# A hybrid attention block with a convolutional feed-forward part: which engine does which copies and subtractions ahead of the feed-forward part

## The chip, the core and the metric

The kernel runs on one core of a Trainium2 chip. A core has TensorE (PE, matrix products), VectorE (DVE), ScalarE (ACT), GpSimd (POOL) and a queue for data transfers (SP). Each engine works through its own list of instructions in order and waits on semaphores where it needs another engine's result. The metric is the device time of one launch in microseconds, as a median of several launches.

## What is computed

One transformer layer on 2048 tokens of width 1024, in fp32. The part that the change touches lies ahead of the second half (the feed-forward part):

```python
h = rmsnorm(x, g_mix) * (1 + scale1) + shift1
a_u, a_v, b_q, b_k, b_v, c_q, c_k, c_v = split(h @ w_in)
y_a = spatial_gating(a_u, a_v)          # gelu, rmsnorm of v, causal 128x128 mix
y_b = stick_breaking(b_q, b_k, b_v)     # 6 heads
y_c = dilated_window(rope(c_q), rope(c_k), c_v)   # 6 heads, dilations 1, 4, 16
x = x + (1 + gate1) * (concat(y_a, y_b, y_c) @ w_out)
# then: h2 = rmsnorm(x), conv(h2 @ w_up), silu(gate) * val, @ w_down, final rmsnorm
```

Stick-breaking, for one query and all keys before it, needs a product from the far end, taken with a scan:

```python
beta = sigmoid(z);  stay = sigmoid(-z)          # both masked: beta 0, stay 1 where key >= query
weight[k] = beta[k] * prod(stay[j] for j > k)   # the stick-breaking product
out = weight @ v
```

## The kernel before

Every fp32 product on TensorE is made of three passes: an operand is split into a rounded high part (`hi`) and the rest (`lo = x - hi`), and hi·hi, hi·lo and lo·hi are added in PSUM (`mm3`, lines 90 to 104). So each weight tile, each normalised activation and each attention weight costs a cast (`copy`, lines 70 to 74) and a subtraction (`tt`, line 78) on some engine besides the matmuls.

Which engine does it is a table, `ENGINES`: each place in the code ("site") has a string of letters, `a` for ScalarE, `v` for VectorE, `p` for GpSimd, and `engine()` goes round that string with each call. `"wlo": "pvv"` puts the first of every three low parts of `w_in` tiles on GpSimd and two on VectorE.

The work goes through these stages:

- 0 to 145 us: the first modulation columns (`ada_first`: `ada_acc` sums on VectorE, line 187), the first normalised tokens (`hh`, `hl`) and the first projections (`whi`, `wlo`).
- 145 to 545 us: projections of the first 1024 tokens, the rotary embedding (`rotate`: `stage*cos`, `stage*sin`, `rot`) and the stick-breaking heads of the first half, interleaved; the spatial gating (`sgu`: `v`, `vs`).
- 545 to 805 us: the same projections of the second half and the dilated-window heads.
- 805 to 1240 us: the stick-breaking heads of the second half, with the output projection of the first half between them (`wo_hi`, `wo_lo`, `yraw`, `yh`, `yl`).
- 1240 us to the end: the rest of the output projection and the feed-forward part.

One step of `stick` on 128 queries and 512 keys: TensorE makes `z`; ScalarE makes `stay` and `beta` by two sigmoids (lines 532, 533); on the diagonal GpSimd masks both (`affine_select`, line 536); VectorE scans `stay` into `excl` (line 540); GpSimd multiplies `beta` by `excl` (site `beta`); TensorE transposes that into PSUM (`tr`, line 546); ScalarE casts it to `wh`, VectorE subtracts to `wl`; TensorE multiplies both with the values (`av`, line 557).

The order of instructions on an engine is that of a scheduler that lays the program out by its own estimates of durations. It is given the table, so a different engine for one site moves instructions on all engines. Inside `run`, side units (`~bqk2`, `~op0` and so on) are mixed into the stick heads by credit; this isn't touched.

Of the kernel before, what the change touches and what calls it, by code (L numbers as in the profile page):

```python
# [43 lines left out]
class Kernel:  # L44
# [16 lines left out]
    def engine(self, site):  # L61

        turns = ENGINES.get(site, site)
        n = self.turn[site] = self.turn.get(site, -1) + 1
# [1077 lines left out]
        self.cp.release()  # L1142


ENGINES = {"whi0": "a", "wlo0": "pppv", "lnt0": "a", "hlo0": "pppv", "lnt": "va", "lnx00": "avv", "lnx01": "aav", "lnx10": "v", "lnx11": "v", "lnx": "va", "hlo": "pvv", "whi": "v", "wlo": "pvv", "qkhi": "avv", "qklo": "v", "cqk": "a", "rot1": "ppv", "rot2": "pv", "rot3": "v", "rothi": "aav", "rotlo": "pvv", "sgu1": "pv", "sgu2": "p", "sguhi": "ap", "sgulo": "ppv", "ya": "aaav", "fold": "a", "beta": "p", "whi_s": "a", "whi_d": "avv", "wom": "v", "wohi": "aav", "wolo": "pv", "ysc": "pv", "yhi": "av", "ylo": "pv", "wuhi": "v", "wulo": "pvv", "wdm": "p", "wdhi": "av", "wdlo": "ppv", "upc": "av", "gv": "pppv", "ghi": "ap", "glo": "ppv", "vhi": "av", "vlo": "v", "uc": "v"}

BUFS = {"gm": 3, "z": 2, "tr": 2, "av": 1, "wraw": 2, "whi": 3, "wlo": 3, "s8": 3, "cs": 2, "tmp2": 2, "khat": 3, "vhat": 2, "q": 2, "beta": 4, "excl": 4, "wh": 2, "wl": 2, "fold": 1, "ys": 1, "x4": 2, "yraw": 2, "ysc": 4, "yh": 2, "yl": 2, "xo": 3, "wuraw": 4, "wul": 3, "wuh": 3, "wdraw": 2, "fx": 2, "up": 3, "dn": 5, "wdh": 2, "wdl": 2, "upc": 3, "cv": 3, "gh": 4, "gl": 4, "fs": 4, "fry": 2, "frr": 2}

# [41 lines left out]
```

## Time and profile before

| | us |
|---|---|
| median of 3 runs (2830.4 to 2834.19) | 2831.44 |
| profiled execution, its own time | 2831.72 |
| span of that execution | 2830.0 |
| PE busy | 2639.5 (93%) |
| DVE busy | 2182.7 (77%) |
| POOL busy | 1197.3 (42%) |
| ACT busy | 987.6 (35%) |

A busy time is summed over the engine's instructions, and a matmul's end is modelled. An instruction that is blocked after it has begun counts as busy all the while, so a duration can be that of the work or that of the work and a stall; the least and the median duration of one shape tell the two apart.

### The profile page before, as it was taken

What the parts mean: (1) busy time and instruction counts of PE and PEld (TensorE: products, weight loads), DVE (VectorE), ACT (ScalarE), POOL (GpSimd) and SP (SyncE); (2) the same over time, 40 slices, a digit from 0 to 9 for tenths busy, and PEclk for the clock granted to TensorE, in tenths of its full rate; (3) what the DMA queues carried; (4) which work ended last, traced back from release to release, by engine and by line L of the source; (5) the groups of instructions that cost most, each with busy time, mean ns of one, the idle gap of its engine ahead of it and who ended that gap; (6) DMA issues with size and microseconds to landing.
All of it is one profiled execution on the core that took longest, in us unless ns stands there. A gap on an engine that the chain in (4) does not pass through costs nothing.

```text
span 2830.0 us, 37108 instructions
## 1 busy us (share of the span) xinstructions
PE 2639.5 (93%) x13334; PEld 2208.6 (78%) x13334; DVE 2182.7 (77%) x3188; ACT 987.6 (35%) x1841; POOL 1197.3 (42%) x1138
## 2 busy tenths in 40 slices
PE   7989899899887888899999999999998999999997
PEld 6868897788866777777788888888877888888886
DVE  5587888766589999964787777777888778777776
ACT  5244444333455666633222112122262212112113
POOL 3276524330158776722444333334444333433323
PEclk9989999999988999999999999999999999999999
DMA  7645485878564332258211111111133111111111
GB/s 233 198 114 164 140 292 173 225 186 215 141 179 127 93 93 66 79 180 297 67 55 50 52 46 45 45 45 53 47 117 119 45 45 60 45 53 45 45 38 60
DMA packets 305300, 309.40 MB, mean 109 GB/s; under 512 B 65516, under 2 KB 245596, under 8 KB 305116
## 3 DMA queue, kind: packets, MB, share of 16 engines
q1 hardware_dynamic: 305116, 307.02, 36.8%
q8 instruction: 106, 1.74, 0.3%
q14 instruction: 78, 0.64, 0.1%
HBM read 232.36 MB, written 68.30 MB: 106 GB/s over the span
## 4 chain that ended last, share of the span: by engine, by line
PE 62%; DVE 15%; DMA 9%; issue 6%; POOL 4%; ACT 3%; SPq 1%; DVEq 0%; POOLq 0%; ACTq 0%
PE up L93 11%; PE up L94 11%; PE up L92 11%; PE dn L94 5%; PE dn L92 5%; PE dn L93 5%; DVE excl L540 3%; PE gmv L342 2%; POOL beta L78 2%; DMA wraw<-in_w_in_dram 2%; PE av L557 2%; SPq L83 1%; DMA wada<-in_w_ada_dram 1%; DVE wl L78 1%; PE tr L546 1%
## 5 line engine op out<-in xcount | busy, mean ns | idle before, releaser
L92 PE MATMUL up<-gh,wuh 128*128 128x512 f32 x1408 | 552.8, 393 | 2.1 <-ACT gh L260 2.1
L94 PE MATMUL up<-gh,wul 128*128 128x512 f32 x1408 | 554.5, 394 | 0.0
L93 PE MATMUL up<-gl,wuh 128*128 128x512 f32 x1408 | 554.3, 394 | 0.0
L821 DVE TENSOR_TENSOR acc<-dn,acc 128x512 f32<-128x512 f32 x688 | 441.4, 681 | 104.3 <-PE dn L94 103.6
L779 DVE SCALAR_TENSOR_TENSOR cv<-upc,cw,cv 128x512 f32<-128x512 f32 x352 | 339.9, 966 | 104.1 <-ACT cv L777 101.0
L78 POOL TENSOR_TENSOR beta<-beta,excl 128x128 f32<-128x128 f32 (+2 forms) x240 | 310.8, 1308 | 140.7 <-DVE excl L540 101.1
L92 PEld LDWEIGHTS up<-gh,wuh 128*128 128x128 f32 x1408 | 264.7, 188 | 62.0 <-ACT gh L260 2.3
L93 PEld LDWEIGHTS up<-gl,wuh 128*128 128x128 f32 x1408 | 265.0, 188 | 61.2 <-issue 0.2
L94 PEld LDWEIGHTS up<-gh,wul 128*128 128x128 f32 x1408 | 264.8, 188 | 59.8 <-issue 0.2
L92 PE MATMUL dn<-wdh,gh 128*128 128x512 f32 x688 | 271.3, 395 | 11.6 <-DVE acc L821 10.4
L93 PE MATMUL dn<-wdl,gh 128*128 128x512 f32 x688 | 271.2, 394 | 0.0
L94 PE MATMUL dn<-wdh,gl 128*128 128x512 f32 x688 | 256.6, 396 | 0.0
L777 ACT ACTIVATE cv<-up,cb 128x512 f32<-128x512 f32 x176 | 136.6, 776 | 284.6 <-DVE upc L72 284.6
L540 DVE TENSOR_TENSOR_SCAN excl<-stay,excl 128x513 f32<-128x513 f32 x144 | 224.6, 1574 | 2.0 <-ACT stay L532 1.9
L70 ACT ACTIVATE upc<-up 128x512 f32<-128x512 f32 x88 | 52.5, 597 | 379.7 <-PE up L94 379.6
L70 ACT ACTIVATE wh<-tr 128x128 fp32r<-128x128 f32 (+2 forms) x240 | 128.5, 541 | 161.2 <-PE tr L546 150.4
L72 DVE CAST wuh<-wuraw 128x512 fp32r<-128x512 f32 x176 | 131.3, 785 | 63.5 <-PE up L93 58.3
L546 PE MATMUL tr<-ident,beta 128*128 128x128 f32 x816 | 139.4, 292 | 37.1 <-POOL beta L78 26.5
L342 PE MATMUL gmv<-wlo,hh 128*128 128x256 f32 x576 | 169.5, 295 | 2.5 <-DVE wlo L78 1.4
L774 POOL COPY upc<-upc 128x2 f32<-128x2 f32 x88 | 20.7, 235 | 353.6 <-DVE upc L72 302.2
L342 PE MATMUL gmv<-whi,hh 128*128 128x256 f32 x576 | 169.0, 294 | 1.3 <-DVE vst L78 1.3
L78 POOL TENSOR_TENSOR wlo<-wraw,whi 128x512 fp32r<-128x512 f32 x35 | 53.4, 1529 | 275.2 <-DVE whi L72 178.3
(249 smaller groups left out, 6092.5 us busy)
## 6 DMA issues: line engine op xcount, KB each, us to landing
wuraw<-in_w_up_dram SPq DMA_DIRECT2D x176, 256.0 KB, 3.2
wdraw<-in_w_down_dram SPq DMA_DIRECT2D x44, 512.0 KB, 3.5
wada<-in_w_ada_dram SPq DMA_DIRECT2D x32, 512.0 KB, 5.7
wraw<-in_w_in_dram SPq DMA_DIRECT2D x112, 128.0 KB, 4.7
vd<-vst SPq DMA_DIRECT2D x12, 1024.0 KB, 5.3
q<-bq SPq DMA_DIRECT2D x48, 256.0 KB, 4.3
q<-cq SPq DMA_DIRECT2D x48, 256.0 KB, 4.2
x<-xo SPq DMA_DIRECT2D x24, 512.0 KB, 6.0
```

Of the source, the lines that this page charges most:

```text
L70: self.nc.scalar.activation(out, in_, AF.Copy)
L72: self.nc.vector.tensor_copy(out, in_)
L78: (self.nc.vector if eng == "v" else self.nc.gpsimd).tensor_tensor(out=out, in0=a, in1=b, op=op)
L92: self.nc.tensor.matmul(ps, ah, bh, start=(k == 0), stop=False)
L93: self.nc.tensor.matmul(ps, ah, bl, start=False, stop=False)
L94: self.nc.tensor.matmul(ps, al, bh, start=False, stop=(k == n - 1))
L342: self.nc.tensor.matmul(ps[:, e, :], a[:, o:o + P], b, start=(n == 0), stop=(n == 3 * KB - 1))
L540: nc.vector.tensor_tensor_scan(x[:, o:513][:, ::-1], sr, sr, 1.0 if diag else carry[j], op0=ALU.mult, op1=ALU.bypass)
L546: nc.tensor.transpose(tr[:, e, :], b[:, o + e * P:o + (e + 1) * P], self.ident)
L777: nc.scalar.activation(t, ps, AF.Identity, bias=self.cb[:, blk:blk + 1], scale=self.cw[2][:, blk:blk + 1])
L779: nc.vector.scalar_tensor_tensor(out=t, in0=u[:, tap:tap + TG], scalar=self.cw[tap][:, blk:blk + 1], in1=t, op0=ALU.mult, op1=ALU.add)
L821: nc.vector.tensor_tensor(out=acc[t][:, ns], in0=ps, in1=acc[t][:, ns], op=ALU.add)
```

## The change

One line of the table is changed. Sites used ahead of the feed-forward part that had some or all of their calls on GpSimd go to VectorE altogether (`wlo0`, `hlo0`, `hlo`, `wlo`, `rot1`, `rot2`, `rotlo`, `sgu1`, `sgu2`, `sgulo`, `wolo`, `ysc`, `ylo`), and two casts to ScalarE (`whi`, which was on VectorE, and `sguhi`). `beta` stays on GpSimd, and so do the masks, which name GpSimd in the code. The sites of the feed-forward part itself (`wulo`, `wdm`, `wdlo`, `gv`, `ghi`, `glo`) stay; `hlo` is also used for the normalised rows that enter it.

```diff
-ENGINES = {"whi0": "a", "wlo0": "pppv", "lnt0": "a", "hlo0": "pppv", ..., "hlo": "pvv", "whi": "v", "wlo": "pvv", ..., "rot1": "ppv", "rot2": "pv", "rot3": "v", "rothi": "aav", "rotlo": "pvv", "sgu1": "pv", "sgu2": "p", "sguhi": "ap", "sgulo": "ppv", ..., "wolo": "pv", "ysc": "pv", "yhi": "av", "ylo": "pv", ...}
+ENGINES = {"whi0": "a", "wlo0": "v", "lnt0": "a", "hlo0": "v", ..., "hlo": "v", "whi": "a", "wlo": "v", ..., "rot1": "v", "rot2": "v", "rot3": "v", "rothi": "aav", "rotlo": "v", "sgu1": "v", "sgu2": "v", "sguhi": "a", "sgulo": "v", ..., "wolo": "v", "ysc": "v", "yhi": "av", "ylo": "v", ...}
```

In all 117 instructions leave GpSimd: 35 `wlo`, 25 `hl` and `gl`, 14 `stage` and 4 `rot` of the rotary embedding, 11 of the spatial gating, 12 `yraw`, 12 `yl` and 4 `wo_lo`. 115 of them come to VectorE and 2 to ScalarE, and 76 casts `whi` go from VectorE to ScalarE.

GpSimd's list in the first half's stick heads, near 210 us (names carry the number of their tile; `cos` is the table of the rotary embedding), before:

```order
L78 TENSOR_TENSOR beta_1611<-beta_1611,excl_1618 128x384
L536 AFFINE_SELECT stay0_676<-stay0_676 128x128
L536 AFFINE_SELECT beta_1630<-beta_1630 128x128
L78 TENSOR_TENSOR beta_1630<-beta_1630,excl_1637 128x512
L78 TENSOR_TENSOR stage_2550<-stage_2550,cos_1403 128x1024
L78 TENSOR_TENSOR beta_1660<-beta_1660,excl_1663 128x512
L78 TENSOR_TENSOR rot_2609<-rot_2609 128x1024
L536 AFFINE_SELECT stay0_676<-stay0_676 128x128
L536 AFFINE_SELECT beta_1715<-beta_1715 128x128
L78 TENSOR_TENSOR beta_1676<-beta_1676,excl_1679 128x512
```

and the same stretch of GpSimd's list now:

```order
L78 TENSOR_TENSOR beta_1611<-beta_1611,excl_1618 128x384
L536 AFFINE_SELECT stay0_676<-stay0_676 128x128
L536 AFFINE_SELECT beta_1630<-beta_1630 128x128
L78 TENSOR_TENSOR beta_1630<-beta_1630,excl_1637 128x512
L78 TENSOR_TENSOR beta_1660<-beta_1660,excl_1663 128x512
L78 TENSOR_TENSOR beta_1676<-beta_1676,excl_1679 128x512
L536 AFFINE_SELECT stay0_676<-stay0_676 128x128
```

The two 1024-wide instructions that stood between the products of one group are gone, and its three products follow each other.

VectorE's list where the output projection's weights are made, near 835 us (`excl` is the scan, `wl` the low part of the attention weights), before:

```order
L540 SCALAR_TENSOR_TENSOR excl_8872<-stay1_678,excl_8827 128x513
L78 TENSOR_TENSOR woraw_8535<-woraw_8535,gate2_8518 128x1024
L78 TENSOR_TENSOR wl_8765<-tr_8798,wh_8764 128x4x128
L78 TENSOR_TENSOR yraw_8637<-ycraw_8650,yscale_8649 128x4x64
L540 SCALAR_TENSOR_TENSOR excl_8888<-stay2_680,excl_8843 128x513
L78 TENSOR_TENSOR wl_8820<-tr_8830,wh_8819 128x4x128
L78 TENSOR_TENSOR wl_8820<-tr_8846,wh_8819 128x4x128
L78 TENSOR_TENSOR wo_lo1_8539<-woraw_8535,wo_hi1_8538 128x1024
L540 SCALAR_TENSOR_TENSOR excl_8935<-stay0_676 128x129
```

and from the same scan on now:

```order
L540 SCALAR_TENSOR_TENSOR excl_8872<-stay1_678,excl_8827 128x513
L78 TENSOR_TENSOR woraw_8535<-woraw_8535,gate2_8518 128x1024
L78 TENSOR_TENSOR wl_8765<-tr_8798,wh_8764 128x4x128
L78 TENSOR_TENSOR yraw_8637<-ycraw_8650,yscale_8649 128x4x64
L540 SCALAR_TENSOR_TENSOR excl_8888<-stay2_680,excl_8843 128x513
L78 TENSOR_TENSOR wo_lo0_8532<-woraw_8528,wo_hi0_8531 128x1024
L78 TENSOR_TENSOR wl_8820<-tr_8830,wh_8819 128x4x128
L540 SCALAR_TENSOR_TENSOR excl_8935<-stay0_676 128x129
L78 TENSOR_TENSOR wl_8820<-tr_8846,wh_8819 128x4x128
L540 SCALAR_TENSOR_TENSOR excl_8952<-stay1_678 128x257
L78 TENSOR_TENSOR wo_lo1_8539<-woraw_8535,wo_hi1_8538 128x1024
```

`wo_lo0`, which GpSimd made, now stands in VectorE's list behind a scan and ahead of the `wl` that the next `av` matmuls need.

ScalarE's list in the first stick heads (a piece of the difference, with + for now and - for before; `whi` is a cast of a `w_in` tile, `wh` the cast of the transposed attention weights):

```order
+L70 ACTIVATE whi<-wraw 128x512 x2
+L70 ACTIVATE wh<-tr 128x2x128
+L533 ACTIVATE beta<-z 128x256
+L70 ACTIVATE wh<-tr 128x3x128
+L532 ACTIVATE stay_676<-z 128x512
+L533 ACTIVATE beta<-z 128x512
+L70 ACTIVATE whi<-wraw 128x512 x2
+L532 ACTIVATE stay_678<-z 128x512
```

The casts of the weights now stand in pairs between the sigmoids and the `wh` casts of the stick heads.

## Rows read from the trace of the kernel before

**Rows 1.** Windows: stretch, length, busy of PE, PEld, DVE, ACT, POOL; clock, DMA, GB/s.

```profile
0.00:145.00 145.00, 121.21 (x635) 103.12 (x636) 85.28 (x136) 57.56 (x99) 45.29 (x92) 0.98 0.70 211
145.00:545.00 400.00, 361.74 (x2347) 328.68 (x2346) 325.88 (x457) 169.12 (x327) 197.14 (x169) 0.95 0.62 186
545.00:805.00 260.00, 233.76 (x1530) 211.88 (x1529) 163.15 (x435) 102.47 (x263) 47.21 (x38) 0.95 0.67 172
805.00:1240.00 435.00, 368.62 (x2060) 302.28 (x2060) 388.05 (x411) 258.90 (x530) 310.70 (x285) 0.93 0.38 105
1240.00:2830.00 1590.00, 1554.20 (x6768) 1262.59 (x6766) 1220.39 (x1750) 399.55 (x624) 596.97 (x555) 0.99 0.23 72
```

**Rows 2.** The same for the inner part of the fourth stretch.

```profile
845.00:1200.00 355.00, 301.94 (x1723) 249.03 (x1724) 330.30 (x348) 224.69 (x462) 269.86 (x248) 0.94 0.33 93
```

**Rows 3.** PE's waits, 805 to 1240 us: us in total, times, longest.

```profile
PE tr L546 <- POOL beta L78: 26.5, 34, 2.2
PE av L557 <- DVE wl L78: 22.7, 20, 2.6
```

**Rows 4.** Instruction groups of POOL, 145 to 545 us: busy us, mean ns | idle before.

```profile
L78 POOL TENSOR_TENSOR wlo<-wraw,whi 128x512 fp32r<-128x512 f32 x15 | 23.3, 1550 | 82.1 <-DVE whi L72 60.6 <-PE z L528 10.3 <-DMA stage<-stage 5.9
L78 POOL TENSOR_TENSOR stage<-stage,cos 128x1024 f32<-128x1024 f32 x7 | 21.4, 3053 | 15.8 <-DMA stage<-stage 8.1 <-ACT cos L381 7.7
...
L78 POOL TENSOR_TENSOR stage<-stage,sin 128x1024 f32<-128x1024 f32 x5 | 14.0, 2801 | 19.6 <-DMA q<-cq 15.7 <-DMA stage<-stage 3.9
```

**Rows 5.** The group of DVE that goes to ACT, 145 to 545 us.

```profile
L72 DVE CAST whi<-wraw 128x512 fp32r<-128x512 f32 x43 | 30.8, 741 | 1.4 <-DMA wraw<-in_w_in_dram 1.4
```

**Rows 6.** The cast that ACT does already, whole span.

```profile
L70 ACT ACTIVATE whi<-wraw 128x512 fp32r<-128x512 f32 x12 | 7.2, 626 | 16.4 <-DMA wraw<-in_w_in_dram 16.3
```

**Rows 7.** Three tiles' instructions on DVE, whole span: ns least/median/most, first and last start.

```profile
L78 DVE TENSOR_TENSOR wlo<-wraw,whi x53: 658/681/2260, 31.4 to 775.5; 128x512 fp32r<-128x512 f32 x53
...
L72 DVE CAST whi<-wraw x76: 394/426/2635, 98.2 to 775.2; 128x512 fp32r<-128x512 f32 x76
...
L78 DVE TENSOR_TENSOR stage<-stage,sin x6: 1187/1266/2830, 174.5 to 593.6; 128x1024 f32<-128x1024 f32 x6
```

**Rows 8.** Timeline, DVE and POOL, 8 to 60 us: start us, us.

```profile
14.75 0.75 DVE L187 SCALAR_TENSOR_TENSOR ada_acc<-wada,cact,ada_acc 128x512 f32<-128x512 f32 x1
...
20.47 11.05 DVE L187 SCALAR_TENSOR_TENSOR ada_acc<-wada,cact,ada_acc 128x512 f32<-128x512 f32 x7
...
19.26 4.18 POOL L78 TENSOR_TENSOR wlo<-wraw,whi 128x512 fp32r<-128x512 f32 x3 [13.51 <-ACT whi L70]
```

**Rows 9.** Chain of waits: start us, us, what.

```profile
209.99 4.89 POOL stage L78
...
791.27 2.41 POOL v L78
```

**Rows 10.** Instruction groups of POOL that move, 805 to 1240 us.

```profile
L78 POOL TENSOR_TENSOR yraw<-ycraw,yscale 128x256 f32<-128x256 f32 x11 | 16.4, 1493 | 23.4 <-DVE yl L78 15.2 <-DMA yscale<-scd 6.1 <-issue 1.2
...
L78 POOL TENSOR_TENSOR yl<-yraw,yh 128x1024 fp32r<-128x1024 f32 x4 | 11.4, 2851 | 0.0
L78 POOL TENSOR_TENSOR wo_lo<-woraw,wo_hi 128x1024 fp32r<-128x1024 f32 x4 | 10.9, 2720 | 0.6 <-DVE wo_hi L72 0.6
```

**Rows 11.** Instruction groups of DVE, 805 to 1240 us.

```profile
L540 DVE TENSOR_TENSOR_SCAN excl<-stay,excl 128x513 f32<-128x513 f32 x120 | 189.8, 1597 | 0.2 <-ACT stay L532 0.2
...
L78 DVE TENSOR_TENSOR yraw<-ycraw,yscale 128x256 f32<-128x256 f32 x10 | 9.4, 938 | 0.0
...
L78 DVE TENSOR_TENSOR wo_lo<-woraw,wo_hi 128x1024 fp32r<-128x1024 f32 x4 | 7.4, 1856 | 0.0
...
L78 DVE TENSOR_TENSOR yl<-yraw,yh 128x1024 fp32r<-128x1024 f32 x4 | 5.7, 1433 | 0.0
```

**Rows 12.** Tile `excl`, 805 to 1240 us: ns least/median/most.

```profile
L78 POOL TENSOR_TENSOR beta<-beta,excl x168: 408/1096/2493, 811.6 to 1213.0; 128x512 f32<-128x512 f32 x132, 128x128 f32<-128x128 f32 x12, 128x256 f32<-128x256 f32 x12, 128x384 f32<-128x384 f32 x12
L540 DVE TENSOR_TENSOR_SCAN excl<-stay,excl x120: 1252/1506/3386, 812.1 to 1211.5; 128x513 f32<-128x513 f32 x120
```

More of the change, by code (lines that the diff above doesn't have):

```diff
@@ L1142, in run @@
         self.cp.release()
-ENGINES = {"whi0": "a", "wlo0": "pppv", "lnt0": "a", "hlo0": "pppv", "lnt": "va", "lnx00": "avv", "lnx01": "aav", "lnx10": "v", "lnx11": "v", "lnx": "va", "hlo": "pvv", "whi": "v", "wlo": "pvv", "qkhi": "avv", "qklo": "v", "cqk": "a", "rot1": "ppv", "rot2": "pv", "rot3": "v", "rothi": "aav", "rotlo": "pvv", "sgu1": "pv", "sgu2": "p", "sguhi": "ap", "sgulo": "ppv", "ya": "aaav", "fold": "a", "beta": "p", "whi_s": "a", "whi_d": "avv", "wom": "v", "wohi": "aav", "wolo": "pv", "ysc": "pv", "yhi": "av", "ylo": "pv", "wuhi": "v", "wulo": "pvv", "wdm": "p", "wdhi": "av", "wdlo": "ppv", "upc": "av", "gv": "pppv", "ghi": "ap", "glo": "ppv", "vhi": "av", "vlo": "v", "uc": "v"}
+ENGINES = {"whi0": "a", "wlo0": "v", "lnt0": "a", "hlo0": "v", "lnt": "va", "lnx00": "avv", "lnx01": "aav", "lnx10": "v", "lnx11": "v", "lnx": "va", "hlo": "v", "whi": "a", "wlo": "v", "qkhi": "avv", "qklo": "v", "cqk": "a", "rot1": "v", "rot2": "v", "rot3": "v", "rothi": "aav", "rotlo": "v", "sgu1": "v", "sgu2": "v", "sguhi": "a", "sgulo": "v", "ya": "aaav", "fold": "a", "beta": "p", "whi_s": "a", "whi_d": "avv", "wom": "v", "wohi": "aav", "wolo": "v", "ysc": "v", "yhi": "av", "ylo": "v", "wuhi": "v", "wulo": "pvv", "wdm": "p", "wdhi": "av", "wdlo": "ppv", "upc": "av", "gv": "pppv", "ghi": "ap", "glo": "ppv", "vhi": "av", "vlo": "v", "uc": "v"}
 BUFS = {"gm": 3, "z": 2, "tr": 2, "av": 1, "wraw": 2, "whi": 3, "wlo": 3, "s8": 3, "cs": 2, "tmp2": 2, "khat": 3, "vhat": 2, "q": 2, "beta": 4, "excl": 4, "wh": 2, "wl": 2, "fold": 1, "ys": 1, "x4": 2, "yraw": 2, "ysc": 4, "yh": 2, "yl": 2, "xo": 3, "wuraw": 4, "wul": 3, "wuh": 3, "wdraw": 2, "fx": 2, "up": 3, "dn": 5, "wdh": 2, "wdl": 2, "upc": 3, "cv": 3, "gh": 4, "gl": 4, "fs": 4, "fry": 2, "frr": 2}
```

## The prediction

> **What bounds the kernel now.** I read first the busy time of the engines by stretch [rows 1]. After 1240 us TensorE is busy for 1554 of 1590 us: matmuls bound that half, and nothing in it but eleven `gl` is moved. Ahead of it TensorE is idle for 24, 38, 26 and 66 us in the four stretches (length less busy time), 154 us together. That is the most that the change can win at the clock granted there; in the fourth stretch that clock is 0.93 of 2.4 GHz.
>
> Then the waits of TensorE in the fourth stretch [rows 3]: 26.5 us for GpSimd's product `beta`, 22.7 us for VectorE's `wl`. So one engine that loses work and one that gains work hold TensorE up about equally. The inner part shows how full they are: VectorE is busy for 330 of 355 us (93%), GpSimd for 270 (76%) [rows 2]. In the second stretch VectorE is busy for 326 of 400 us, GpSimd for 197, ScalarE for 169 [rows 1].
>
> Last I read durations, since "busy" hides stalls here. One `ada_acc` sum takes 0.75 us alone, and seven take 11.05 us, 1.58 each, while GpSimd runs its `wlo` and `hl` [rows 8]. The cast `whi` has a median of 426 ns over the whole span and a mean of 741 in the second stretch, where GpSimd is busiest beside it [rows 5, 7]. The scan has a least time of 1252 ns and a mean of 1597 [rows 11, 12]. So VectorE stalls where GpSimd works, by about 0.83 us for one GpSimd instruction (1.58 less 0.75).
>
> **The change, stretch by stretch.** I price moved instructions on VectorE at their medians there: 0.68 us for 128x512 (`wlo`), 1.27 for 128x1024 (`stage*sin`), against 1.55, 2.80 and 3.05 on GpSimd [rows 4, 7]. Each moved instruction so gets its own result earlier by 0.9 to 1.8 us, and takes room in the fuller queue.
>
> Second stretch. 42 instructions leave GpSimd. VectorE gets 15 `wlo` and 5 `hl` at 0.68 (13.6 us) and 21 of 1024 columns (7 and 5 `stage`, 4 `rot`, 5 of the gating) at 1.27 (26.7 us): +40. The 43 casts leave it: -31 [rows 5]. ScalarE takes them at 0.626 us each, +27 us on 169 of 400 [rows 1, 6]. Stalls: I take that half of the 42 met a VectorE instruction and cost 0.83 us: 42 x 0.83 / 2 = -17. VectorE's load: 326 + 40 - 31 - 17 = 318, slightly less. The chain of waits runs through moved GpSimd work, as the 4.89 us `stage` [rows 9]; at 1.27/2.80 it keeps 45%, -2.7 for this one. I take -6 for the stretch: 2.7, and 3.3 as some 40% of the 8 us off VectorE's load, since TensorE at 362 of 400 covers the rest. Bounds: if all stalls and waits in the moved work go, -22 (17 + 4.9); if none do and the 9 us net of moved work (40 - 31) is all on the path, +9.
>
> First stretch. 9 `wlo` and 6 `hl` of GpSimd's 45 us [rows 1] are within the turns of the sites that move, at 0.68 each +10 on VectorE; fewer than half of 15 x 0.83 = 12 us of stalls went with them. The seven `ada_acc` lost 11.05 - 7 x 0.75 = 5.8 us to seven instructions that would cost 4.8 on VectorE. A tie; results come earlier, and I take -2, bounds -6 and +6.
>
> Third stretch. Some 8 `wlo` and 6 of the rotation and gating come to VectorE (8 x 0.68 + 6 x 1.27 = 13 us), some 24 casts leave it (76 in all [rows 7], 43 in the second stretch, about 9 in the first), 24 x 0.43 = 10. The gating's `v` is on the chain with 2.41 us on GpSimd [rows 9], and `vs` follows it; each halves. -3, bounds -6 and +4.
>
> Fourth stretch. GpSimd loses `yraw`, `yl`, `wo_lo`, 16.4 + 11.4 + 10.9 = 38.7 of 310.7 us, 12% [rows 1, 10]. VectorE gets 11 + 4 + 4 of them, at its own means 10.3 + 5.7 + 7.4 = 23 us, with two narrower `yl` 25 [rows 11]; without stalls I put it at 17. I take 20. Back comes part of the scans' stalls: 120 x (1597 - 1252) ns = 41 us in all; 12% of that is 5, and if every moved instruction stalled VectorE, 8 wide ones by the longest scan's 2.13 us (3386 - 1252) and 11 by 0.83, it is 26. I take 12. At 93% on the path: (20 - 12) x 0.93 = +7. GpSimd's queue is shorter, so the 26.5 us wait for `beta` falls by 12% or somewhat more, -4. Sum +3; bounds -17 (17 added, 26 stalls and 8 of the wait gone) and +25 (nothing comes back). Queued behind the added `wo_lo`, `yl` and `yraw` are scans and `wl`, and TensorE's transposes and `av` wait for these.
>
> ScalarE: 76 casts x 0.626 = +48 us on 588 us busy in 1240 [rows 1, 6]. They hide beside TensorE, but each waits on ScalarE for its transfer (16.4 us idle before 12 casts [rows 6]), with sigmoids and `wh` behind it; before, the scans stood behind such a wait on VectorE. +1, bounds -5 and +12. Feed-forward part: eleven `gl`, as wide as a `wlo`, from about 1.4 (4.18/3 [rows 8]) to 0.7 us; TensorE doesn't wait for them: 0.
>
> Sum: -2 - 6 - 3 + 3 + 1 = -7 us on 2830.0 span and 1.7 around it (2831.7, the profiled execution; the median of the runs shown is 2831.4): 2824.5, rounded to **2824 us**.
>
> The Trainium skill bears on the stall: "SBUF — State Buffer", § Who interferes with whom, says that VectorE with two SBUF inputs and GpSimd reading SBUF share a port by an exclusive lock, held for the whole instruction. The rows on `ada_acc` show the stall, but less of it: 0.83 us to a `wlo` of 1.39 us (4.18/3). By the rule every moved instruction gives its whole GpSimd time back where the port is full; what that makes of the time is the first rival.
>
> **Rivals.**
>
> 1. GpSimd and VectorE take turns in the fourth stretch, and their sum is the bound. For: 132 products at 1.10 us and 120 scans at 1.25 are 145 + 150 = 295 of 435 us before any other work on the two [rows 12]. Against: the product at 1.10 beside `wl` from PSUM shows that some of both overlaps. Then 38.7 us leave the turn and 17 to 25 enter: -14 to -22, and the second stretch wins its bound, -22. With -2, -3 and +1: 2831.7 - 18 - 22 - 4 = 2788; half of it on the path, 2810.
>
> 2. VectorE becomes the bound. Place: 845 to 1020 us and on, with 93% already. Price: +25 in the fourth stretch, +9 in the second, as no stalls come back, because products stall the scans as before. It decides as soon as less than about 13 of 41 us of the scans' stalls return. Time 2831.7 + 25 + 9 - 5 + 1 = 2862; half on the path, 2846.
>
> 3. The sums cancel and the time stays within 0.2% (5.7 us, about what a measurement of this kernel tells from no change). TensorE's 362 of 400 and 234 of 260 us [rows 1] cover what the queues win.
>
> 4. ScalarE's casts hold sigmoids up behind late transfers: +12, 2836 by my other terms. That the change doesn't do what it says is excluded by the lists of instructions: ahead of the feed-forward part GpSimd keeps products and masks alone.
>
> **How the numbers follow.** A moderate win about my sum, 6 to 18 us: 0.29. Rival 1, more than that: 0.19. Rival 3: 0.21. Rival 2: 0.20; rival 4: 0.11; both slower by over 0.2%, together 0.31. So faster is 0.48, same 0.21, slower 0.31. The likeliest case's own range is 2813 to 2826. The whole range goes to the half-weight of rivals 1 and 2 and a little beyond on the cheap side: 2798 to 2848.
>
> **What would show it.** Right: `whi` gone from VectorE; mean scan in the fourth stretch down from 1597 to about 1500 ns; the wait for `beta` below 23 us; VectorE's busy time in 145 to 545 us at about 318; the fourth stretch within 10 us of 435. Wrong: the feed-forward part begins later than 1240 us with VectorE over 95% and TensorE's wait for `wl` above 35 us (rival 2), or begins before 1215 us (rival 1); ScalarE idle before `whi` and TensorE waiting for `wh` (rival 4).

## The result and the profile after

The changed kernel takes 2801.3 us (median of 4 runs, 2798.09 to 2808.42) against 2830.92 us before on the same chip. The ratio is 0.9899, with a 95% interval of 0.9876 to 0.9922: faster by 29.6 us. The profiled execution took 2798.09 us, with a span of 2796.4, against 2831.72 and 2830.0.

To see where the 33.6 us between the two spans lie, both are cut at the same work: at the first load of the dilated heads' `zc` (line 612), at the first gate product (`gate_ps`, line 224, where the output projection begins) and at the first `up` product (line 92). The first windows are those of the kernel before, the second those of the changed one; the columns are those of [rows 1].

```profile
0.00:473.40 473.40, 418.49 (x2577) 373.82 (x2578) 355.11 (x491) 203.74 (x367) 221.75 (x247) 0.96 0.60 183
473.40:823.10 349.70, 311.69 (x2002) 280.14 (x2000) 233.01 (x554) 137.98 (x346) 80.46 (x66) 0.95 0.73 193
823.10:1322.70 499.60, 431.52 (x2341) 352.80 (x2342) 421.75 (x473) 274.58 (x548) 313.84 (x285) 0.95 0.44 129
1322.70:2830.00 1507.30, 1477.84 (x6419) 1201.80 (x6417) 1172.87 (x1673) 371.30 (x581) 581.26 (x541) 0.99 0.19 60
```

```profile
0.00:478.40 478.40, 422.43 (x2626) 377.34 (x2626) 351.29 (x511) 235.24 (x420) 124.26 (x192) 0.96 0.63 189
478.40:793.00 314.60, 291.05 (x1952) 263.76 (x1952) 211.64 (x533) 152.99 (x373) 37.18 (x42) 0.97 0.77 202
793.00:1293.50 500.50, 432.64 (x2340) 352.33 (x2341) 420.90 (x504) 274.52 (x550) 282.68 (x256) 0.95 0.43 128
1293.50:2796.40 1502.90, 1477.41 (x6419) 1201.18 (x6417) 1172.66 (x1681) 370.74 (x582) 569.48 (x533) 0.99 0.19 61
```

The lengths change by +5.0, -35.1, +0.9 and -4.4 us. The last cut differs by the eleven moved `gl`, and its gain is not all scatter: over the fourteen profiles of this study it takes 1502.0 to 1505.5 us (mean 1502.9) in the eight kernels that have every `gl` on VectorE, and 1504.7 to 1507.3 us (mean 1505.9) in the six that do not. The rest, 30.1 us, is won before the first gate product, 823.1 against 793.0 us, and nearly all of that in the stretch of the second half's projections and dilated heads. Some 50 of that stretch's matmuls now run ahead of the cut, which is one reason why the first line is longer; up to the gate product both kernels issue the same 4577 matmuls. The next two windows run from the start to there, before and after:

```profile
0.00:823.10 823.10, 730.18 (x4577) 653.96 (x4577) 588.12 (x1044) 341.72 (x713) 302.21 (x313) 0.95 0.66 187
```

```profile
0.00:793.00 793.00, 713.48 (x4577) 641.11 (x4577) 562.93 (x1043) 388.23 (x793) 161.45 (x234) 0.97 0.69 194
```

TensorE's idle time falls from 92.9 to 79.5 us (-13.4), and the same 4577 matmuls are busy for 16.7 us less, at a granted clock of 0.97 instead of 0.95 of 2.4 GHz, the upper of its two levels (1.2 and 2.4 GHz). So over half of the difference stands in TensorE's busy time. That is a way of counting and not a cause: a lower busy time can come back as idle time, as the rotation alone shows below. VectorE, which got 115 instructions (most of them here) and gave 76 away, is busy for 25 us less.

Part of why VectorE has room shows in the first 60 us. GpSimd runs nothing from 6 to 125 us of the changed kernel. The rows answer to [rows 8]: the `ada_acc` sums and the moved `wlo`, `hl` on VectorE in the changed kernel (timeline: start, us), and then all 28 sums of that width before and after.

```profile
20.46 1.28 DVE L78 TENSOR_TENSOR wlo<-wraw,whi 128x512 fp32r<-128x512 f32 x2
21.66 0.74 DVE L187 SCALAR_TENSOR_TENSOR ada_acc<-wada,cact,ada_acc 128x512 f32<-128x512 f32 x1
22.33 0.68 DVE L78 TENSOR_TENSOR hl<-ln_tmp,hh 128x512 fp32r<-128x512 f32 x1
22.93 0.74 DVE L187 SCALAR_TENSOR_TENSOR ada_acc<-wada,cact,ada_acc 128x512 f32<-128x512 f32 x1
```

```profile
L187 DVE SCALAR_TENSOR_TENSOR ada_acc<-wada,cact,ada_acc 128x512 f32<-128x512 f32 x28 | 30.3, 1081 | 1.1 <-DMA wada<-in_w_ada_dram 0.5
L187 DVE SCALAR_TENSOR_TENSOR ada_acc<-wada,cact,ada_acc 128x512 f32<-128x512 f32 x28 | 20.9, 748 | 0.4 <-DMA wada<-in_w_ada_dram 0.2
```

A sum takes 0.74 us beside a silent GpSimd; seven in a row took 1.58 each beside its `wlo` and `hl`. The moved instructions are interleaved with the sums and fill the time that the stalls took.

In the third cut (the fourth stretch of the prediction) much moved and nothing was won. These are groups of VectorE in the changed kernel from 775 to 1206 us, and then the scan by its tile there; they answer to [rows 11] and [rows 12].

```profile
L78 DVE TENSOR_TENSOR yraw<-ycraw,yscale 128x256 f32<-128x256 f32 x21 | 17.8, 869 | 4.0 <-DMA ycraw<-yc 4.0
L78 DVE TENSOR_TENSOR yl<-yraw,yh 128x1024 fp32r<-128x1024 f32 x8 | 9.8, 1227 | 0.0
L78 DVE TENSOR_TENSOR wo_lo<-woraw,wo_hi 128x1024 fp32r<-128x1024 f32 x8 | 9.7, 1209 | 0.0
```

```profile
L78 POOL TENSOR_TENSOR beta<-beta,excl x168: 412/1102/6822, 782.4 to 1178.8; 128x512 f32<-128x512 f32 x132, 128x128 f32<-128x128 f32 x12, 128x256 f32<-128x256 f32 x12, 128x384 f32<-128x384 f32 x12
L540 DVE TENSOR_TENSOR_SCAN excl<-stay,excl x120: 1250/1320/2128, 782.9 to 1177.3; 128x513 f32<-128x513 f32 x120
```

The scan's median falls from 1506 to 1320 ns and its longest from 3386 to 2128; a 1024-wide `wo_lo` from 1856 to 1209 on the average. VectorE does twice as many of these for the same 421 us. But the longest product on GpSimd is now 6822 ns instead of 2493: GpSimd is the one that is kept waiting longest. Its 128x512 products take 1542 ns on the average from 793 to 1293 us of the changed kernel, and 1459 in the same stretch before. The longest is one of the two in the first of the next rows; VectorE works without a gap beside it, at `yl`, `wo_lo` and scans:

```profile
830.51 7.83 POOL L78 TENSOR_TENSOR beta<-beta,excl 128x512 f32<-128x512 f32 x2 [2.32 <-DVE excl L540]
830.94 1.20 DVE L78 TENSOR_TENSOR yl<-yraw,yh 128x1024 fp32r<-128x1024 f32 x1
832.07 0.94 DVE L540 TENSOR_TENSOR_SCAN excl<-stay 128x385 f32<-128x385 f32 x1
832.94 1.19 DVE L78 TENSOR_TENSOR wo_lo<-woraw,wo_hi 128x1024 fp32r<-128x1024 f32 x1
834.05 1.21 DVE L540 TENSOR_TENSOR_SCAN excl<-stay 128x513 f32<-128x513 f32 x1
835.19 1.19 DVE L78 TENSOR_TENSOR wo_lo<-woraw,wo_hi 128x1024 fp32r<-128x1024 f32 x1
```

TensorE's wait for GpSimd's products is as before, from 775 to 1206 us of the changed kernel (us, times, longest; answers to [rows 3]):

```profile
PE tr L546 <- POOL beta L78: 26.5, 40, 2.0
PE av L557 <- DVE wl L78: 18.3, 18, 1.9
```

### The profile page after: what moved, and what is told of

Same layout as the page of the kernel before. It is cut to its first block, busy times and chain, and to the rows that moved or that the text cites. A ratio compares the mean times of both kernels' runs of the same rounds, so it can differ in the third digit from the quotient of the medians.

```text
span 2796.4 us, 37076 instructions
## 1 busy us (share of the span) xinstructions
PE 2623.5 (94%) x13334; PEld 2194.6 (78%) x13334; DVE 2156.5 (77%) x3227; ACT 1033.5 (37%) x1922; POOL 1013.6 (36%) x1021
## 4 chain that ended last, share of the span: by engine, by line
PE 65%; DVE 12%; DMA 9%; issue 6%; ACT 4%; POOL 3%; SPq 1%; DVEq 0%; POOLq 0%; ACTq 0%
PE up L93 11%; PE up L92 11%; PE up L94 11%; PE dn L94 5%; PE dn L92 5%; PE dn L93 5%; DVE excl L540 3%; PE gmv L342 2%; POOL beta L78 2%; PE av L557 2%; DMA wada<-in_w_ada_dram 2%; SPq L83 1%; PE tr L546 1%; PE gm L101 1%; DVE wl L78 1%
## 5 line engine op out<-in xcount | busy, mean ns | idle before, releaser
L78 POOL TENSOR_TENSOR beta<-beta,excl 128x128 f32<-128x128 f32 (+2 forms) x240 | 331.3, 1393 | 173.3 <-DVE excl L540 118.9
L536 POOL TENSOR_SCALAR_AFFINE_SELECT stay<-stay 128x128 f32<-128x128 f32 x96 | 58.1, 606 | 527.8 <-ACT stay L532 401.9
L540 DVE TENSOR_TENSOR_SCAN excl<-stay,excl 128x513 f32<-128x513 f32 x144 | 212.2, 1484 | 4.8 <-ACT stay L532 4.8
L342 PE MATMUL gmv<-whi,hl 128*128 128x256 f32 x576 | 166.9, 291 | 3.9 <-DVE hl L78 3.9
```

The lines of the kernel that those rows point to most:

```text
L78: (self.nc.vector if eng == "v" else self.nc.gpsimd).tensor_tensor(out=out, in0=a, in1=b, op=op)
L342: self.nc.tensor.matmul(ps[:, e, :], a[:, o:o + P], b, start=(n == 0), stop=(n == 3 * KB - 1))
L536: nc.gpsimd.affine_select(out=t[:, 384:512], in_=t[:, 384:512], pattern=[[-1, P]], compare_op=ALU.is_gt, fill=fill, base=0, channel_multip ...
L540: nc.vector.tensor_tensor_scan(x[:, o:513][:, ::-1], sr, sr, 1.0 if diag else carry[j], op0=ALU.mult, op1=ALU.bypass)
```

## The experiments

Each kernel changes entries of `ENGINES` and nothing else, so each computes the same. The ratio is to the kernel before on the same chip. A profile is one execution. Of each two lengths are told: to the first gate product (before 823.1 us, changed 793.0) and from there to the first `up` product (499.6 and 500.5).

**The cast alone.**

```diff
-"whi": "v"
+"whi": "a"
```

> The kernel before with one site changed: the casts whi go from VectorE to ScalarE, everything on GpSimd stays. Theory A (the cast held VectorE's list up behind late weight transfers, as in the 9.41 us at 544 us, and nothing else counts much): most of the gain of the whole change, 2805 to 2815 us, and the fall lies between 475 and 605 us. Theory B (GpSimd's work is what counts, by the shared stalls and its list): 2825 to 2833. Theory C (any new order of the lists moves the time by some 20 us either way): anything from 2805 to 2850.

2825.97 us, ratio 0.9994 (0.9985 to 1.0004): no gain, so theory A falls. Lengths 821.8 and 497.9. In the kernel before, VectorE's list did stand still behind a late transfer (from its timeline):

```profile
553.72 0.43 DVE L72 CAST whi<-wraw 128x512 fp32r<-128x512 f32 x1 [9.41 <-DMA wraw<-in_w_in_dram]
```

but taking this wait to another engine wins nothing by itself. A likely reason is that the wait does not leave VectorE's list: the low part `wlo` there needs the cast, and now waits for ScalarE about as long as the cast waited for its transfer (us, times, longest; 145 to 820 us, before and with the cast moved):

```profile
DVE whi L72 <- DMA wraw<-in_w_in_dram: 22.9, 11, 9.4
DVE wlo L78 <- ACT whi L70: 22.2, 10, 6.3
```

From the start to the first gate product of this kernel:

```profile
0.00:821.80 821.80, 725.01 (x4578) 648.37 (x4578) 549.52 (x969) 385.63 (x791) 304.88 (x313) 0.96 0.66 188
```

VectorE is busy for 39 us less than before and TensorE idle for 97 us instead of 93: VectorE's room is there, and the gate product comes only 1.3 us earlier.

**All but the cast.**

```diff
 # the changed table, with
-"whi": "a"
+"whi": "v"
```

> The whole change but for whi, which stays on VectorE. Theory A: little is left, 2820 to 2835 us, perhaps slower since VectorE gets all of GpSimd's work and keeps the casts. Theory B: 2800 to 2810, nearly the whole gain. If both parts are needed (room on VectorE for what leaves GpSimd), this is slower than 2831 and whi alone gains little.

2808.45 us, 0.9938 (0.9923 to 0.9953): about two thirds of the gain. Lengths 803.7 and 501.6. Neither A (2820 to 2835) nor "both are needed" (slower) holds. B's range (2800 to 2810) holds the time, but a third of the gain is missing. From the start to the first gate product of this kernel:

```profile
0.00:803.70 803.70, 722.47 (x4571) 649.57 (x4572) 587.18 (x1118) 341.29 (x710) 155.66 (x230) 0.95 0.67 193
```

This is the plainest row on the stalls: VectorE does 74 instructions more than before, at least 50 us at 0.68 us each, and is busy for 587.2 us instead of 588.1. So some 50 us of VectorE's busy time before were stalls, and they went as GpSimd's busy time fell from 302 to 156 us.

**The rotation alone.**

```diff
-"rot1": "ppv", "rot2": "pv", "rotlo": "pvv"
+"rot1": "v", "rot2": "v", "rotlo": "v"
```

> The kernel before with the rotary embedding alone (rot1, rot2, rotlo) moved from GpSimd to VectorE: 18 instructions of 1024 columns. Theory B in the form that the rotation's long GpSimd instructions hold up keys and the heads behind them between 475 and 605 us: 2808 to 2818. Theory A: 2826 to 2836.

2825.08 us, 0.9992 (0.998 to 1.0004). Lengths 820.9 and 500.9. No gain clear of the noise: theory B in this form misses by 7 us or more. From the start to the first gate product:

```profile
0.00:820.90 820.90, 722.83 (x4577) 646.63 (x4577) 591.38 (x1062) 344.75 (x715) 257.14 (x295) 0.96 0.67 188
```

TensorE is busy for 7.4 us less than before with the same matmuls and idle for 5.2 us more (98.1), so most of what its busy time lost came back as idle time.

**The low parts alone.**

```diff
-"wlo0": "pppv", "hlo0": "pppv", "hlo": "pvv", "wlo": "pvv"
+"wlo0": "v", "hlo0": "v", "hlo": "v", "wlo": "v"
```

> The kernel before with the low parts of weights and activations alone (wlo0, hlo0, wlo, hlo) moved from GpSimd to VectorE: 60 instructions of 512 columns. Theory B in the form that short GpSimd instructions stall VectorE more than they cost it: 2820 to 2828. Theory A: 2828 to 2838, as VectorE has more behind the waiting casts.

2829.47 us, 1.0004 (0.9992 to 1.0017). Lengths 823.4 and 497.7. No gain either, with GpSimd's busy time to the gate product down to 231 us:

```profile
0.00:823.40 823.40, 727.40 (x4577) 648.68 (x4578) 594.78 (x1092) 343.42 (x714) 230.91 (x262) 0.95 0.66 187
```

**The gating alone.**

```diff
-"sgu1": "pv", "sgu2": "p", "sguhi": "ap", "sgulo": "ppv"
+"sgu1": "v", "sgu2": "v", "sguhi": "a", "sgulo": "v"
```

> The kernel before with the spatial gating alone moved (sgu1, sgu2, sgulo to VectorE, sguhi to ScalarE). By the runs so far the whole change but whi gains 0.6%, the rotation alone and the low parts alone nothing. Theory D (the parts add up, so the gain of all but whi sits in what is still untried): 2808 to 2818. Theory E (GpSimd's one list couples rotation, weights and gating, so no family gains by itself, and the gain comes when all of them leave it): 2824 to 2832. Theory C (order alone): anything.

2823.27 us, 0.9989 (0.9976 to 1.0001). Lengths 819.5 and 500.9. The four families alone add up to ratios 0.0006, 0.0008, -0.0004 and 0.0011 below one, 0.0021 together, against 0.0101 for the whole. (The output projection was not moved alone; taken back out of the whole it costs 0.0009, below.) Theory D, that the parts add up, falls.

**Other turns, as many on GpSimd.**

```diff
-"wlo": "pvv", "rot1": "ppv", "rot2": "pv", "ysc": "pv", "ylo": "pv", "wolo": "pv"
+"wlo": "vpv", "rot1": "vpp", "rot2": "vp", "ysc": "vp", "ylo": "vp", "wolo": "vp"
```

> The kernel before with the turns of six sites shifted (wlo vpv, rot1 vpp, rot2 vp, ysc vp, ylo vp, wolo vp): as many instructions on GpSimd as before, but other ones, so that all lists come out in another order. Theory C (a new order alone moves the time by as much as the change did): 15 to 30 us off 2829 either way. Theories B, D and E (what counts is what leaves GpSimd): within 6 us of 2829.

2830.38 us, 1.0007 (0.9994 to 1.0021). Lengths 821.6 and 498.1. One other order of all lists moves the time by less than 0.25%. This is a single order, so theory C is made unlikely for a 1% win, not excluded.

**The changed kernel with one family back.** The rotation:

```diff
-"rot1": "v", "rot2": "v", "rotlo": "v"
+"rot1": "ppv", "rot2": "pv", "rotlo": "pvv"
```

> The changed kernel with the rotation's sites back as before (18 instructions of 1024 columns on GpSimd again). Theory E with the rotation as the part that the others need: 2818 to 2830, most of the gain lost. If the rotation doesn't count: 2799 to 2805.

2808.11 us, 0.9926 (0.9908 to 0.9944). Lengths 802.3 and 499.2. Some 7 us are lost, though the intervals of the two kernels overlap; it is less than theory E's form with the rotation as the needed part expected.

The gating:

```diff
-"sgu1": "v", "sgu2": "v", "sguhi": "a", "sgulo": "v"
+"sgu1": "pv", "sgu2": "p", "sguhi": "ap", "sgulo": "ppv"
```

> The changed kernel with the spatial gating's sites back as before. So far: whi, rotation, low parts and gating alone gain 0 to 5 us each, the whole 28; without whi or without the rotation 20 are left. Theory E (several families share GpSimd's list, each that stays takes back a part): 2805 to 2814. If the gating alone were needed by all others: 2820 to 2830. If it doesn't count: 2799 to 2804.

2805.53 us, 0.9918 (0.9904 to 0.9931). Lengths 796.8 and 493.7. By the ratio 0.2% of the time is lost, within the intervals of both.

The low parts:

```diff
-"wlo0": "v", "hlo0": "v", "hlo": "v", "wlo": "v"
+"wlo0": "pppv", "hlo0": "pppv", "hlo": "pvv", "wlo": "pvv"
```

> The changed kernel with the low parts (wlo0, hlo0, wlo, hlo) back on their turns with GpSimd; whi on ScalarE, rotation, gating and output projection moved. Theory E: 2805 to 2815. Theory F (the weights' low parts are the core: a wlo on GpSimd stands in one list with the stick products and frees the raw weight tile late, and every other family only adds): 2818 to 2830. If they don't count: 2799 to 2804.

2812.82 us, 0.9936 (0.9923 to 0.9948). Lengths 806.3 and 499.9. Together with the cast's this is the largest loss of a single part, but no core that all the rest hangs on (theory F).

The output projection:

```diff
-"wolo": "v", "ysc": "v", "ylo": "v"
+"wolo": "pv", "ysc": "pv", "ylo": "pv"
```

> The changed kernel with the output projection's sites (wolo, ysc, ylo) back as before. In the trace after, the stretch from the first gate product to the first up product takes 500.5 us against 499.6 before, so what left GpSimd there has bought nothing: 2797 to 2805, within 4 us of the changed kernel. If GpSimd's shorter list did gain there and something else took it, 2806 to 2815; if VectorE's added work costs, 2788 to 2796.

2801.93 us, 0.9908 (0.9889 to 0.9928): the time of the changed kernel. From its first gate to its first `up` product:

```profile
800.90:1299.00 498.10, 427.64 (x2340) 350.86 (x2341) 423.88 (x476) 275.96 (x551) 309.13 (x284) 0.96 0.44 129
```

VectorE is busy for 423.9 us with 476 instructions and for 420.9 with 504 when it does them all: what moves there pays for itself in stalls and wins nothing.

**Two families.**

```diff
 # the table before, with
-"wlo0": "pppv", "hlo0": "pppv", "hlo": "pvv", "wlo": "pvv", "sgu1": "pv", "sgu2": "p", "sguhi": "ap", "sgulo": "ppv"
+"wlo0": "v", "hlo0": "v", "hlo": "v", "wlo": "v", "sgu1": "v", "sgu2": "v", "sguhi": "a", "sgulo": "v"
```

> The kernel before with low parts and gating moved, the two families that both kernels with 20 us of gain have in common (alone they gained 0 and 5 us, within their intervals). Theory F, with the two as the core: 2806 to 2814. Theory E: 2816 to 2826, more than the sum of the two alone and less than with a third family.

2823.05 us, 0.9975 (0.9964 to 0.9986). Lengths 818.6 and 499.8. As theory E expected: more than the two alone (0.0007 together), and far from the 20 us of a core.

All fourteen profiles, ordered by GpSimd's busy time up to the first gate product (us), with the time of that product:

| cast `whi` on | GpSimd busy: first gate product |
|---|---|
| VectorE | 303: 821.6 (other turns); 302: 823.1 (before); 277: 819.5 (gating); 257: 820.9 (rotation); 231: 823.4 (low parts); 202: 818.6 (two families); 156: 803.7 (all) |
| ScalarE | 305: 821.8 (cast alone); 233: 806.3 (low parts back); 208: 802.3 (rotation back); 188: 796.8 (gating back); 165: 800.9 (output projection back); 161: 793.0 (changed); 159: 797.2 (the last experiment, next) |

The last three of the second row have the same work ahead of the gate product and lie 7.9 us apart, so steps of that size are not told from scatter here. With the cast on ScalarE the gate product comes about 2 us earlier for each 10 us off GpSimd, (821.8 - 793.0) / (305 - 161) = 0.2. With it on VectorE the first 100 us bring 4.5 us and the last 46 bring 14.9.

What is clear of the noise, the cast's step only just, is that parts are worth more together than alone. The cast gains 0.06% alone and 0.39% on top of everything else (0.9938 to 0.9899). The rotation gains 0.08% alone and 0.37% on top of the two families (0.9975 to 0.9938; the output projection moves with it, which taken back costs 0.09%). Neither is a condition of the rest: with the cast still on VectorE the others win 0.62%. Why the parts help each other was only argued, by the room on VectorE and by the lists that all of them share; which wait links them was not isolated.

**One step further.** By the profiles VectorE is the busiest engine beside TensorE in the output projection's stretch, so two more casts there go to ScalarE.

```diff
 # the changed table, with
-"yhi": "av", "wohi": "aav"
+"yhi": "a", "wohi": "a"
```

> The changed kernel with the casts yhi and wohi of the output projection wholly on ScalarE; before, half of the first and two of eight of the second were on VectorE: by the trace after, 5.3 + 3.2 + 2.3 us of VectorE's 420 in the 500 us from the first gate product to the first up product. If VectorE's list bounds that stretch (331.7 of 355 us busy in it): 2791 to 2796 us and a stretch of 490 to 495. If the turn-taking of products and scans bounds it, the casts count there too, a little less: 2794 to 2799. If the latency of one product, transpose, cast and subtraction after another bounds it: 2799 to 2804.

2790.59 us, ratio 0.9861 (0.9838 to 0.9883): 39 us faster than before and some 10 faster than the changed kernel, whose interval it touches only at the edge. The win lies in the stretch where it was expected, and is a little larger than expected:

```profile
797.20:1284.60 487.40, 423.28 (x2343) 346.95 (x2342) 409.49 (x490) 284.17 (x564) 273.72 (x254) 0.97 0.45 132
```

That is 13.1 us shorter than in the changed kernel, with VectorE busy for 11.4 us less (420.9 to 409.5), and shorter than in all thirteen other profiles (493.7 to 501.6 us). It speaks for VectorE's list as the bound and does not prove it. Of the 13.1 us, 9.4 stand in TensorE's busy time (432.6 to 423.3), and TensorE's wait for VectorE's `wl` did not fall (18.3 to 20.3 us), while that for GpSimd's product did (25.2 to 20.8). It is the fastest version of this study.

## Why the prediction was right, and where it was not

The sign and the range (2798 to 2848) held; the size did not: 7 us were forecast, 29.6 came. That the range held was in part luck. It reached down to 2798 for the sake of rival 1, which came nearer with its 2810 and 2788 but put the win in the fourth stretch, where nothing was won. (The sum itself is 2831.7 - 7 = 2824.7, not 2824.5.)

- **Stalls of VectorE behind GpSimd: right.** I took 0.83 us for an overlapped instruction. The sum on `ada_acc` fell by just that, 1.58 to 0.74, and the scans' mean in the fourth stretch to near the 1500 ns that I had named (1506 over the same 120 scans from 775 to 1206 us, 1597 before).
- **First stretch, -2 us: not borne out.** The last of its products at line 315 starts at 114.0 us instead of 111.3.
- **Second stretch, VectorE at about 318 us: right**, 321.7 over the same 145 to 545 us, with 369 of TensorE's time in it instead of 362. In time the first two stretches won less than the 8 us I gave them: 49 more matmuls run before the first cut, some 9 us at the 0.18 us of a matmul with its idle time there (473.4 / 2577), and the cut is 5.0 us later. By this estimate 4 us are won.
- **Third stretch, -3 us: this step failed.** I costed it by VectorE's load (13 us in, 10 us out) and the halving of one wait of the gating, and let no stall of VectorE come back there. Up to the gate product my terms for VectorE's load come to about -5 us (a tie, -8 and +3); it fell by 25.2. From the first `zc` to the gate product TensorE's idle time fell from 38.0 to 23.6 us, while ahead of that it stayed (54.9 and 56.0). The clock had no term either: up to the gate product 16.7 us stand in the busy time of the same matmuls and 13.4 in idle time. Which waits ended there was not isolated.
- **The parts as a sum: failed.** I added the stretches' terms and the cast's as if each stood by itself. The cast alone is worth 0.06%, GpSimd's families 0.15% together when each goes alone, and the whole 1.01%.
- **Fourth stretch, +3 us: +0.9 came, but by luck.** The 3 us were +7 for VectorE's list and -4 for TensorE's wait for the product, and neither came. VectorE's added work came back wholly (421.8 to 420.9 us) instead of 12 of 20: 10.5 us of it in the scans (189.8 to 179.3), and some in `yraw`, `yl` and `wo_lo`, each shorter than the same instruction on VectorE before. TensorE's wait didn't fall below 23 us as I expected; it stayed at 26.5, with longer products on GpSimd.
- **The feed-forward part, 0:** about 3 us seem to be won there (a last cut of 1505.9 us in the mean of the kernels that keep `gl` on GpSimd's turns, 1502.9 with all of them moved). I took it that TensorE doesn't wait for `gl`; how the time is won is open.
- **My sign for rival 1**, a feed-forward part that begins before 1215 us, came up for another reason: the first `up` product comes 29.2 us earlier (1240 less 29.2 is 1211), all of it won ahead of the fourth stretch.
- **Rival 2** had the wrong price: its 25 us came back. Its bound, VectorE, may be right: in the last experiment, taking 11.4 us off VectorE went with a stretch 13.1 us shorter. That is one profile, and two profiles whose tables agree on that stretch lie up to 6.8 us apart there (500.5 and 493.7).
- **ScalarE, +1 us: not contradicted.** It waits much more for weights, 76 us before the 88 casts of the changed kernel, instead of 16.4 before 12 [rows 6], and TensorE does not wait more for it: its waits for ScalarE up to the gate product add up to 10.8 us, against 13.5 before. VectorE does wait for the casts, 43.0 us before its `wlo` up to the gate product, much as in the run with the cast alone. The row is ScalarE's group over 0 to 793 us:

```profile
L70 ACT ACTIVATE whi<-wraw 128x512 fp32r<-128x512 f32 x88 | 53.1, 628 | 108.7 <-DMA wraw<-in_w_in_dram 76.1 <-PE gm L101 16.5 <-PE gmv L342 6.1
```

- **The port.** The rule of the Trainium skill that I set beside the stall ("SBUF — State Buffer", § Who interferes with whom: the second of the two to start is blocked) agrees with the trace after in that both sides are seen to stall: with GpSimd silent a sum takes 0.74 us, and beside VectorE's wide instructions a product takes up to 6.8. In size it does not: a sum lost 0.83 us to a `wlo` of 1.39, as the prediction said. My rival 1 read from it that the freed time must shorten the fourth stretch. It did not; VectorE's list there came out as long as before.

## What to carry to other kernels

An engine's busy time before a change can hold stalls: 9.4 of 30.3 us in the 28 sums here, and some 50 of 588 us on VectorE up to the gate product. So price moved work at the least duration on the engine that gets it, and take back the stalls that it caused where it was; here the two cancelled. Parts that share in-order lists need not add: a part that wins nothing clear alone (the cast, the rotation) can be worth 0.4% on top of the others, so test a change by taking parts out of it as well as by putting one in. And when the matrix engine's busy time falls at a higher granted clock, look whether its idle time rose, before you count the fall as won.

## What was not expected of the hardware

With the same 4577 matmuls TensorE's busy time fell by 16.7 us (730.2 to 713.5) as the granted clock rose from 0.95 to 0.97 and its idle time fell by 13.4. With the rotation alone it fell by 7.4 us, at 0.96, and 5.2 us of that came back as idle time. And the stalls between VectorE and GpSimd changed sides: the longest scan went from 3386 to 2128 ns, the longest product from 2493 to 6822, while the busy time of VectorE in that stretch moved by less than 1 us.
